# Scores of 64 queries by 192 keys with reversed sign, the sink as a 129th column, and decay factors from one maximum and four exponentials, in a two-layer hybrid attention and state-space trunk

## The chip, the cores and the metric

The kernel runs on one core of one Trainium2 chip. The metric is device time in microseconds (us), the median of the runs of one kernel. The engines are called as in the profile: PE is TensorE (matmuls), PEld its weight loads, DVE is VectorE, ACT is ScalarE, POOL is GpSimd, SP is SyncE, which issues all of this kernel's transfers.

## The reference, cut to what matters

One sequence of 2048 tokens of width 1024 goes through two layers. In each layer sixteen query heads (four key/value heads) attend to the last 128 tokens, with a learned sink in the softmax, beside a Mamba-2 scan in chunks of 128 tokens; both are gated and projected together.

```python
scores = jnp.einsum("bnqkgd,bnskd->bnkgqs", q, kb) * (HEAD_DIM ** -0.5)
scores = scores - slopes * dist                      # 128 queries x 256 keys, 128 of them valid
scores = jnp.where(valid, scores, -jnp.inf)
m = jnp.maximum(scores.max(axis=-1, keepdims=True), sink)
p = jnp.exp(scores - m)
probs = p / (p.sum(axis=-1, keepdims=True) + jnp.exp(sink - m))
out = jnp.einsum("bnkgqs,bnskd->bnqkgd", probs, vb)
attn = out * jax.nn.silu(z_attn)
...
diff = a_cs[..., :, None] - a_cs[..., None, :]       # a_cs: running sum of dt * a in a chunk
decay = jnp.exp(jnp.where(tril, diff, -jnp.inf))
y_diag = einsum(cb, decay, xdt)                      # per head, 128 x 128 decay factors
```

## The kernel before, in words

The work runs over 2 layers, 4 chunks of 512 tokens and 2 halves of the heads. A half has, in the order of the code, the key projection (`stage_k`), for each of its two key/value heads the query and gate projections (`proj_a`) and the attention (`mix_a`), the projections of the state-space group (`proj_s`), the output projection of the attention (`out_proj`) and the scan (`mix_s`); the output projection of the scan (`tail`) is put off until after the next `proj_a`. Numbers are split into a high and a low float32r part, so each projection is three matmuls of 512 columns (L229 to L231, L237 to L239, L448 to L450). The order on each engine is not written out by hand: a scheduler interleaves these stages when the program is built, and the engines then run their lists in that order.

`mix_a` works on blocks of 128 queries for four heads. There are 128 such blocks in the program. The scores of two heads go into one PSUM bank (`ps_s`; there is one buffer of it): per head two matmuls of 256 columns, the block's own 128 keys and the 128 before them (L376, L377). ACT copies the older half of both heads to an SBUF tile `e` (`s4`, L380) and DVE writes over it where the newer key is the valid one (L381), so that the 128 valid keys share 128 columns. Then DVE adds the distance term and takes the row maximum, head by head (L384), a small DVE operation forms the negated maximum with the sink (`nm`, L387), another the sink's distance from it (`es`, L389), ACT exponentiates that (L390) and the four heads (L393, with row sums `den`), DVE adds the sink's part to the sum (L395), inverts it (L396) and scales the tile (L397). PE transposes the four heads into `ps_pt` (L401); POOL separates the older from the newer keys (L409, L412), and four matmuls of 512 columns form the output (L416 to L419), which is gated by `zs` (L428, two operations).

`mix_s` works on 64 blocks. For each of two groups of four heads it loads the running sums of a block, one row per head, to all 128 partitions (L537, from the DRAM tile `a`, 2 KB to a partition), subtracts each partition's own sum and cuts at zero (L540, four operations on DVE), exponentiates (L542, one operation of 512 elements on ACT) and multiplies by `cbm` (L544, the first group on DVE and the second on POOL); `ps_yd` (L549) is the matmul that uses it. The tiles `e` of `mix_a` and `mix_s` share four buffers.

In the first layer's first chunk, weights are split as they come and stored; from the second chunk of the first layer on, `w_ahead` splits the weights of the second layer between other work (L103 on DVE, `whi` and `wr`).

Of the kernel before, what the change touches and what calls it, by code (L numbers as in the profile page):

```python
# [24 lines left out]
U8 = mybir.dt.uint8  # L25
# [28 lines left out]
def trunk(ctx, tc, a):  # L54
# [194 lines left out]
    def stage_vdt(L, lc, c, banks):  # L249
# [50 lines left out]
        nc.vector.tensor_copy(out=at, in_=ps[0:64, 128:256])  # L300
# [22 lines left out]
    def silu2(ps, name, pool, tag, bufs):  # L323
        th = tp.tile([P, 512], F32, name="th", bufs=1)
        nc.scalar.activation(out=th, in_=ps, func=AF.Tanh, scale=0.5)
        z = pool.tile([P, 512], F32, name=name, tag=tag, bufs=bufs)
# [3 lines left out]
    def proj_a(L, kv, X):  # L330
        qs, zs = [], []
        for j in range(2):
            ps = bank(ps_cm, "ps_q")
            proj_cm(X, L, 2 + kv * 2 + j, ps)
            q = ap_.tile([P, 2, CH], F32R, name="q", bufs=3)
            qf = q.bitcast(F32)
            u, v = slice(0, 64), slice(64, 128)
            nc.scalar.activation(out=q[u, 0], in_=ps[u], func=AF.Copy, scale=0.125)
            nc.scalar.activation(out=q[v, 1], in_=ps[v], func=AF.Copy, scale=0.125)
            nc.vector.scalar_tensor_tensor(out=q[v, 0], in0=ps[u], scalar=0.125, in1=qf[u, 0],  # L340
                                           op0=ALU.mult, op1=ALU.subtract)
            nc.vector.scalar_tensor_tensor(out=q[u, 1], in0=ps[v], scalar=0.125, in1=qf[v, 1],
                                           op0=ALU.mult, op1=ALU.subtract)
            qs.append(q)
        for j in range(2):
            ps = bank(ps_cm, "ps_z")
            proj_cm(X, L, 10 + kv * 2 + j, ps)
            zs.append(silu2(ps, "zsa", ap_, "zsa", 4))
# [9 lines left out]
    def mix_a(L, lc, c, kv, vr, vprev, kt, qs, zs, mixt):  # L358
        bias = ap_.tile([P, 4, P], F32, name="bias", bufs=1)
# [3 lines left out]
        for b in range(NB):  # L363
            first = c == 0 and b == 0
            s4 = tp.tile([P, 4, P], F32, name="e4", bufs=E4)
            if first:
                nc.gpsimd.memset(s4, NEG)
            blk = slice(b * P, (b + 1) * P)
            for j in range(2):
                ps = bank(ps_mx, "ps_s").rearrange("p (h u k) -> p h u k", h=2, u=2)  # L370
                for i in range(2):
                    if first:
                        ko, ks = ps[:, i, 1, :], slice(P, 2 * P)
                    else:
                        ko, ks = ps[:, i].rearrange("p u k -> p (u k)"), slice(b * P, b * P + 2 * P)
# [424 lines left out]
```

## Time and profile before

| | |
|---|---|
| time, median of 3 runs | 3267.14 us (3261.64 to 3271.08) |
| time of the profiled execution | 3269.05 us |
| its span, first to last instruction | 3267.3 us |
| busy: PE, PEld | 3133.6 us (96%), 2595.4 us (79%) |
| busy: DVE, ACT, POOL | 2315.4 us (71%), 1330.2 us (41%), 1187.6 us (36%) |
| mean granted TensorE clock | 0.984 |
| moved by DMA | 692.78 MB, mean 212 GB/s |

The span lies 1.75 us below the execution's own time. A busy share is an average over the whole span; matmuls overlap one another in the pipeline, so the busy time of PE holds some waiting too.

### The profile page before, as it was taken

How to read it: one execution, taken by the hardware profiler on the slowest of the kernel's cores; microseconds unless marked ns; L12 is line 12 of the kernel's file. 1: busy time of each engine (PE TensorE's matmuls, PEld its weight loads, DVE VectorE, ACT ScalarE, POOL GpSimd, SP SyncE). 2: the span in 40 equal slices, each digit the busy share in tenths (PEclk: the TensorE clock that was granted, in tenths of full speed). 3: DMA queues.
4: the chain of work that ended last, by engine and by line, in shares of the span. 5: the costliest groups of instructions: out<-in, count | busy, mean ns of one | idle time of the engine just before them, and what ended most of it. 6: DMA issues, size and time to landing. Idle time of an engine off the chain costs nothing.

```text
span 3267.3 us, 46525 instructions
## 1 busy us (share of the span) xinstructions
PE 3133.6 (96%) x15448; PEld 2595.4 (79%) x15448; DVE 2315.4 (71%) x5535; ACT 1330.2 (41%) x3607; POOL 1187.6 (36%) x1327
## 2 busy tenths in 40 slices
PE   9999899999999999999999999999999999999996
PEld 7788787787877878777888888887888878888885
DVE  6978778767687676876759666685766847678575
ACT  5646425344254442543424344252432425334341
POOL 2443442415334142441325414333253322444224
PEclk9999999999999999999999999999999999999997
DMA  8766769757698576985666455654457544565451
GB/s 305 232 244 229 249 223 306 258 172 260 220 296 279 179 233 222 308 288 185 217 194 224 155 173 187 200 197 164 161 191 233 172 157 163 182 228 171 158 198 66
DMA packets 261360, 692.78 MB, mean 212 GB/s; under 512 B 28928, under 2 KB 50176, under 8 KB 261120
## 3 DMA queue, kind: packets, MB, share of 16 engines
q1 hardware_dynamic: 261120, 689.82, 63.5%
q8 instruction: 122, 2.00, 0.3%
q14 instruction: 118, 0.97, 0.1%
HBM read 554.96 MB, written 134.74 MB: 211 GB/s over the span
## 4 chain that ended last, share of the span: by engine, by line
PE 55%; DVE 10%; DMA 9%; POOL 2%; issue 2%; ACT 2%; SPq 0%; DVEq 0%; ACTq 0%; POOLq 0%
PE ps_out L448 5%; PE ps_out L450 5%; PE ps_out L449 5%; PE ps_xbc L230 3%; PE ps_xbc L231 3%; PE ps_xbc L229 3%; DMA e<-a 2%; PE ps_yd L549 2%; PE ps_zs L237 2%; PE ps_zs L238 2%; PE ps_z L231 2%; PE ps_z L229 2%; PE ps_zs L239 2%; PE ps_z L230 2%; DMA wpair<-wd_o 2%
## 5 line engine op out<-in xcount | busy, mean ns | idle before, releaser
L448 PE MATMUL ps_out<-wpair,mixt 128*128 128x512 f32 x1008 | 406.3, 409 | 42.1 <-DMA wpair<-wd_o 21.7
L449 PE MATMUL ps_out<-wpair,mixt 128*128 128x512 f32 x1008 | 403.7, 401 | 7.8 <-DVE wpair L103 7.8
L450 PE MATMUL ps_out<-wpair,mixt 128*128 128x512 f32 x1008 | 401.0, 401 | 7.9 <-DVE mixt L103 5.1
L409 POOL TENSOR_SCALAR_AFFINE_SELECT gh<-fh 128x512 fp32r<-128x512 f32 x128 | 91.7, 716 | 619.6 <-ACT fh L98 583.1
L229 PE MATMUL ps_xbc<-xh,wpair 128*128 128x512 f32 x768 | 305.6, 398 | 0.0
L230 PE MATMUL ps_xbc<-xl,wpair 128*128 128x512 f32 x768 | 302.0, 393 | 0.0
L231 PE MATMUL ps_xbc<-xh,wpair 128*128 128x512 f32 x768 | 301.2, 392 | 0.0
L393 ACT ACTIVATE e<-e,nm 128x128 f32<-128x128 f32 x512 | 199.7, 391 | 181.5 <-DVE nm L387 181.1
L448 PEld LDWEIGHTS ps_out<-wpair,mixt 128*128 128x128 f32 x1008 | 194.8, 194 | 97.7 <-DMA wpair<-wd_o 27.2
L450 PEld LDWEIGHTS ps_out<-wpair,mixt 128*128 128x128 f32 x1008 | 195.1, 194 | 54.5 <-DVE mixt L103 7.8
L449 PEld LDWEIGHTS ps_out<-wpair,mixt 128*128 128x128 f32 x1008 | 195.7, 194 | 49.4 <-DVE wpair L103 10.7
L380 ACT COPY e<-ps_s 128x256 f32<-128x256 f32 x240 | 88.6, 369 | 336.0 <-PE ps_s L377 334.1
L540 DVE TENSOR_SCALAR e<-e,nacs 128x128 f32<-128x128 f32 x512 | 168.9, 392 | 73.7 <-DMA e<-a 73.1
L493 DVE SCALAR_TENSOR_TENSOR cacc<-ps_xbc,conv,cacc 128x511 f32<-128x511 f32 (+2 forms) x288 | 213.4, 741 | 9.9 <-ACT cacc L490 8.0
L237 PE MATMUL ps_zs<-wpair,xh 128*128 128x512 f32 x512 | 203.5, 400 | 7.5 <-DMA wpair<-wd_z 7.5
L355 POOL TENSOR_TENSOR vw<-vr,vw 128x64 fp32r<-128x64 f32 x152 | 62.7, 413 | 392.4 <-ACT vw L354 377.2
L239 PE MATMUL ps_zs<-wpair,xl 128*128 128x512 f32 x512 | 202.2, 395 | 0.0
L238 PE MATMUL ps_zs<-wpair,xh 128*128 128x512 f32 x512 | 201.7, 394 | 0.0
L229 PE MATMUL ps_z<-xh,wpair 128*128 128x512 f32 x512 | 201.4, 393 | 0.0
L230 PE MATMUL ps_q<-xl,wpair 128*128 128x512 f32 x512 | 201.3, 393 | 0.0
L231 PE MATMUL ps_z<-xh,wpair 128*128 128x512 f32 x512 | 201.2, 393 | 0.0
L229 PE MATMUL ps_q<-xh,wpair 128*128 128x512 f32 x512 | 201.0, 393 | 0.0
(227 smaller groups left out, 8396.4 us busy)
## 6 DMA issues: line engine op xcount, KB each, us to landing
wpair<-wd_cm SPq DMA_DIRECT2D x420, 512.0 KB, 3.6
wpair<-wd_o SPq DMA_DIRECT2D x221, 512.0 KB, 4.1
wpair<-wd_z SPq DMA_DIRECT2D x112, 512.0 KB, 3.9
e<-a SPq DMA_DIRECT2D x128, 256.0 KB, 4.4
wr<-wcm SPq DMA_DIRECT2D x120, 256.0 KB, 4.5
wd_cm<-wpair SPq DMA_DIRECT2D x60, 512.0 KB, 3.7
wr<-wo SPq DMA_DIRECT2D x64, 256.0 KB, 4.8
wd_o<-wpair SPq DMA_DIRECT2D x32, 512.0 KB, 3.7
```

What stands on the lines that cost most here:

```text
L229: nc.tensor.matmul(out=ps, lhsT=wh[:, s], rhs=xh, start=(k == 0), stop=False)
L230: nc.tensor.matmul(out=ps, lhsT=wh[:, s], rhs=xl, start=False, stop=False)
L231: nc.tensor.matmul(out=ps, lhsT=wl[:, s], rhs=xh, start=False, stop=(k == KT - 1))
L237: nc.tensor.matmul(out=banks[b], lhsT=xh[:, s], rhs=wh, start=(k == 0), stop=False)
L238: nc.tensor.matmul(out=banks[b], lhsT=xh[:, s], rhs=wl, start=False, stop=False)
L239: nc.tensor.matmul(out=banks[b], lhsT=xl[:, s], rhs=wh, start=False, stop=(k == KT - 1))
L393: nc.scalar.activation(out=s4[:, h, :], in_=s4[:, h, :], func=AF.Exp, bias=nm[:, h:h + 1], accum_out=den[:, h:h + 1])
L448: nc.tensor.matmul(out=banks[b], lhsT=mh, rhs=wh, start=(e == 0), stop=False)
L449: nc.tensor.matmul(out=banks[b], lhsT=mh, rhs=wl, start=False, stop=False)
L450: nc.tensor.matmul(out=banks[b], lhsT=ml, rhs=wh, start=False, stop=(e == 3))
L493: nc.vector.scalar_tensor_tensor(out=acc[:, m:], in0=ps[:, 0:CH - m], scalar=cw[:, j:j + 1], in1=acc[:, m:], op0=ALU.mult, op1=ALU.add)
L540: nc.vector.tensor_scalar(out=e4[:, h, :], in0=e4[:, h, :], scalar1=d["nacs"][:, q:q + 1], scalar2=0.0, op0=ALU.add, op1=ALU.min)
```

## The change

Four parts.

1. **Scores.** The queries are scaled by -0.125 and stored so that 64 queries of two heads lie side by side. A matmul then takes 64 queries of two heads (128 columns of weights) against the 192 keys that these queries can reach, where it took 128 queries of one head against 256 keys. There are eight of them a block, as before. A partition of `e` is now one query of one of two heads. Two ACT copies (L387, L388) take the place of one in the second half of the block, since the 64 newest columns there lie first; the masked copy of DVE (L389) covers 64 columns for each of two heads, where it covered 128.
2. **Sink.** `e` gets a 129th column, which POOL fills with the negated sink (L371, 128x4). The scores are negated, so one minimum over 129 columns gives `nm` (L393) and one exponential with scale -1 over 129 columns gives the whole row sum (L397). L387, L389, L390 and L395 of before go.
3. **Gate.** `zs` is one tile of two gates, and the gating one operation of 256 elements (L435) for two of 128.
4. **Decay.** The stored sums are negated. One DVE operation over 512 elements takes the maximum of the loaded sum and the partition's own (L546), and four ACT exponentials of 128 elements, with scale -1 and the partition's sum as bias (L548), take the place of the one without bias. Since rows of `e` are now 129 wide, L544 loads 512 bytes four times to a partition, for 2 KB once.

```diff
-            q = ap_.tile([P, 2, CH], F32R, name="q", bufs=3)
+            q = ap_.tile([P, CH // 64, 2, 64], F32R, name="q", bufs=3)
...
-            s4 = tp.tile([P, 4, P], F32, name="e4", bufs=E4)
+            s5 = tp.tile([P, 4, P + 1], F32, name="e4", bufs=E4)
+            s4 = s5[:, :, 0:P]
...
+            nc.gpsimd.tensor_copy(out=s5[:, :, P:], in_=ns.unsqueeze(2))
             blk = slice(b * P, (b + 1) * P)
-            for j in range(2):
-                ps = bank(ps_mx, "ps_s").rearrange("p (h u k) -> p h u k", h=2, u=2)
-                for i in range(2):
...
-                    nc.tensor.matmul(out=ko, lhsT=qs[j][:, i, blk], rhs=kt[:, 0, ks], start=True, stop=False)
-                    nc.tensor.matmul(out=ko, lhsT=qs[j][:, i, blk], rhs=kt[:, 1, ks], start=False, stop=True)
-                sj = s4[:, 2 * j:2 * j + 2, :]
-                if not first:
-                    nc.scalar.copy(out=sj, in_=ps[:, :, 0, :])
-                nc.vector.copy_predicated(out=sj, mask=low.unsqueeze(1).broadcast_to([P, 2, P]), data=ps[:, :, 1, :])
-            m = sm.tile([P, 4], F32, name="m")
+            sv = s4.rearrange("p (s j) c -> p s j c", s=2)
+            for s in range(2):
+                t0 = b * P + s * 64
+                ps = bank(ps_mx, "ps_s")[:, 0:384].rearrange("p (j k) -> p j k", j=2)
+                o0 = 128 - 64 * s if first else 0
+                for j in range(2):
+                    for part in range(2):
+                        nc.tensor.matmul(out=ps[:, j, o0:], lhsT=qs[j][:, t0 // 64].rearrange("p i q -> p (i q)"),
+                                         rhs=kt[:, part, t0 + o0:t0 + 192], start=(part == 0), stop=(part == 1))
+                own, other = slice(64 * s, 64 * s + 64), slice(64 - 64 * s, 128 - 64 * s)
+                if not first and s == 0:
+                    nc.scalar.copy(out=sv[:, s], in_=ps[:, :, 0:128])
+                elif s == 1:
+                    if not first:
+                        nc.scalar.copy(out=sv[:, s, :, own], in_=ps[:, :, 0:64])
+                    nc.scalar.copy(out=sv[:, s, :, other], in_=ps[:, :, 64:128])
+                nc.vector.copy_predicated(out=sv[:, s, :, own], mask=low.unsqueeze(1).broadcast_to([P, 2, 64]),
+                                          data=ps[:, :, 128:192])
+            nm = sm.tile([P, 4], F32, name="nm")
             for h in range(4):
-                nc.vector.tensor_tensor_reduce(out=s4[:, h, :], in0=s4[:, h, :], in1=bias[:, h, :], scale=1.0,
-                                               scalar=-3.0e38, op0=ALU.add, op1=ALU.max, accum_out=m[:, h:h + 1])
-            nm = sm.tile([P, 4], F32, name="nm")
-            nc.vector.scalar_tensor_tensor(out=nm, in0=m, scalar=-1.0, in1=ns, op0=ALU.mult, op1=ALU.min)
-            es = sm.tile([P, 4], F32, name="es")
-            nc.vector.tensor_tensor(out=es, in0=nm, in1=ns, op=ALU.subtract)
-            nc.scalar.activation(out=es, in_=es, func=AF.Exp)
+                nc.vector.tensor_tensor_reduce(out=s5[:, h, :], in0=s5[:, h, :], in1=bias[:, h, :], scale=1.0,
+                                               scalar=3.0e38, op0=ALU.add, op1=ALU.min, accum_out=nm[:, h:h + 1])
...
-                nc.scalar.activation(out=s4[:, h, :], in_=s4[:, h, :], func=AF.Exp, bias=nm[:, h:h + 1],
+                nc.scalar.activation(out=s5[:, h, :], in_=s5[:, h, :], func=AF.Exp, scale=-1.0, bias=nm[:, h:h + 1],
                                      accum_out=den[:, h:h + 1])
-            nc.vector.tensor_tensor(out=den, in0=den, in1=es, op=ALU.add)
...
-            for j in range(2):
-                nc.vector.tensor_tensor(out=t[:, j, :], in0=t[:, j, :], in1=zs[j][:, blk], op=ALU.mult)
+            nc.vector.tensor_tensor(out=t, in0=t, in1=zs[:, :, blk], op=ALU.mult)
...
-                e4 = tp.tile([P, 4, P], F32, name="e4", bufs=E4)
+                e4 = tp.tile([P, 4, P + 1], F32, name="e4", bufs=E4)[:, :, 0:P]
...
+                nacs = d["nacs"][:, r0:r0 + 4]
+                nc.vector.tensor_tensor(out=e4, in0=e4, in1=nacs.unsqueeze(2).broadcast_to([P, 4, P]), op=ALU.max)
                 for h in range(4):
-                    q = b * 16 + g * 8 + u * 4 + h
-                    nc.vector.tensor_scalar(out=e4[:, h, :], in0=e4[:, h, :],
-                                            scalar1=d["nacs"][:, q:q + 1], scalar2=0.0, op0=ALU.add, op1=ALU.min)
-                nc.scalar.activation(out=e4, in_=e4, func=AF.Exp)
+                    nc.scalar.activation(out=e4[:, h, :], in_=e4[:, h, :], func=AF.Exp, scale=-1.0, bias=nacs[:, h:h + 1])
```

The rest of the diff follows from these: the views in which POOL separates older and newer keys have runs of 64, the views of `ps_o` are rearranged, and the tables of distances and sinks are laid out for the new rows.

The scheduler makes a new order of the whole program. On DVE, a block's softmax in the second half of a state-space projection stands so before (L384 is shown as ISA, its second row reads the row result out; the L103 row is a weight split that has nothing to do with the block):

```order
L381 COPY_PREDICATED e_13405<-low,ps_s 128x256
L384 ISA e_13405,m<-e_13405,bias 128x128
L384 ISA m 128x1
L384 ISA e_13405,m<-e_13405,bias 128x128
L384 ISA m 128x1
L387 SCALAR_TENSOR_TENSOR nm<-m,nsink 128x4
L103 TENSOR_TENSOR wr<-wr,whi 128x512
L389 TENSOR_TENSOR es<-nm,nsink 128x4
L395 TENSOR_TENSOR den<-den,es 128x4
L396 RECIPROCAL den<-den 128x4
L397 SCALAR_TENSOR_TENSOR e_13405<-e_13405,den 128x512
```

and so in the changed kernel:

```order
L389 COPY_PREDICATED e_13142<-low,ps_s 128x2x64
L393 ISA e_13142,nm<-e_13142,bias 128x129
L393 ISA nm 128x1
L393 ISA e_13142,nm<-e_13142,bias 128x129
L393 ISA nm 128x1
L103 TENSOR_TENSOR wr<-wr,whi 128x512
L399 RECIPROCAL den<-den 128x4
L400 SCALAR_TENSOR_TENSOR e_13142<-e_13142,den 128x4x128
```

Three small operations are gone, and only the weight split still stands between the row result and the reciprocal.

On ACT, the decay factors of a block stand so before (L98 are casts of the scan and of the next output projection's input, L587 the sum of squares of the scan's output):

```order
L430 CAST mixt<-yy 128x256
L542 ACTIVATE e_26460<-e_26460 128x512
L542 ACTIVATE e_26468<-e_26468 128x512
L98 CAST fh<-xx 128x512
L587 ACTIVATE th,ssq<-yy 128x512
L98 CAST gh<-st_103 128x512
```

and so in the changed kernel, at a like place:

```order
L98 CAST fh<-xx 128x512
L548 ACTIVATE e_23986<-e_23986,nacs 128x128 x4
L548 ACTIVATE e_23994<-e_23994,nacs 128x128 x4
L593 ACTIVATE th,ssq<-yy 128x512
L98 CAST gh<-st_104 128x512
L98 CAST mixt<-ps_g 128x512
```

Eight short calls stand where two long ones stood, ahead of the same casts.

On PE, a group of four score matmuls stands within a state-space projection before:

```order
L376 MATMUL ps_s<-kt,q 128x256
L417 MATMUL ps_o<-gl,vw 64x512
L377 MATMUL ps_s<-kt,q 128x256
L376 MATMUL ps_s<-kt,q 128x256
L377 MATMUL ps_s<-kt,q 128x256
L231 MATMUL ps_xbc<-xh_12200,wpair 128x512
```

and in the changed kernel:

```order
L380 MATMUL ps_s<-kt,q 128x192 x2
L424 MATMUL ps_o<-gl,vw 64x512
L380 MATMUL ps_s<-kt,q 128x192 x2
L229 MATMUL ps_xbc<-xh_3752,wpair 128x512
L230 MATMUL ps_xbc<-xl_3753,wpair 128x512
```

The groups are as long as before, with 192 columns for 256. What lies between them has moved: counted over the 128 blocks, the median number of matmuls between a block's last score matmul and its first transposition is 50 before and 42 in the changed kernel.

## Rows read from the trace of the kernel before

**Rows 1.** Page, part 1: busy time, share of the span, instructions.

```profile
PE 3133.6 (96%) x15448; PEld 2595.4 (79%) x15448; DVE 2315.4 (71%) x5535; ACT 1330.2 (41%) x3607; POOL 1187.6 (36%) x1327
```

**Rows 2.** Cores: span and mean granted TensorE clock.

```profile
core 0: 3267.3 us, clock 0.984
```

**Rows 3.** Windows: length, busy PE, PEld, DVE, ACT, POOL (instructions), clock, DMA share, GB/s.

```profile
900.00:1300.00 400.00, 377.40 (x1816) 310.46 (x1815) 278.41 (x680) 165.76 (x436) 131.29 (x149) 0.97 0.73 243
2100.00:2500.00 400.00, 394.31 (x1986) 329.86 (x1985) 277.26 (x697) 154.53 (x437) 150.12 (x171) 1.00 0.56 183
```

**Rows 4.** Waits of PE: total us, times, longest us.

```profile
PE ps_out L448 <- DMA wpair<-wd_o: 21.7, 19, 3.3
PE ps_out L449 <- DVE wpair L103: 7.8, 6, 2.8
PE ps_out L448 <- ACT mixt L98: 7.7, 8, 3.0
...
PE ps_pt L401 <- DVE e L397: 5.6, 11, 1.0
...
PE ps_q L231 <- DVE wpair L103: 0.2, 1, 0.2
PE ps_out L448 <- ACT wpair L98: 0.2, 1, 0.2
```

**Rows 5.** Timeline of PE around a score group of 256 columns: start us, us, instruction.

```profile
457.43 0.28 PE L376 MATMUL ps_s<-kt,q 128*128 128x256 f32 x1
...
457.90 0.40 PE L229 MATMUL ps_q<-xh,wpair 128*128 128x512 f32 x1
458.14 0.40 PE L230 MATMUL ps_q<-xl,wpair 128*128 128x512 f32 x1
```

**Rows 6.** Timeline of PE around a first block's group, of 128 columns.

```profile
39.98 0.22 PE L376 MATMUL ps_s<-kt,q 128*128 128x128 f32 x1
...
40.66 0.40 PE L230 MATMUL ps_q<-xl,wpair 128*128 128x512 f32 x1
```

**Rows 7.** Timeline of the weight loads of that group.

```profile
40.09 0.19 PEld L376 LDWEIGHTS ps_s<-kt,q 128*128 128x128 f32 x1
40.20 0.19 PEld L377 LDWEIGHTS ps_s<-kt,q 128*128 128x128 f32 x1
```

**Rows 8.** Groups of DVE by form: count, busy us, mean ns, idle before.

```profile
L540 DVE TENSOR_SCALAR e<-e,nacs 128x128 f32<-128x128 f32 x512 | 168.9, 392 | 73.7 <-DMA e<-a 73.1
L381 DVE COPY_PREDICATED e<-low,ps_s 128x256 f32<-128x256 uint8 x256 | 112.7, 440 | 67.0 <-ACT e L380 62.9 <-PE ps_s L377 1.2
...
L428 DVE TENSOR_TENSOR yy<-yy,zsa 128x128 f32<-128x128 f32 x256 | 76.5, 340 | 0.9
...
L544 DVE TENSOR_TENSOR e<-e,cbm 128x512 f32<-128x512 f32 x64 | 48.9, 764 | 2.5 <-ACT e L542 2.1
...
L389 DVE TENSOR_TENSOR es<-nm,nsink 128x4 f32<-128x4 f32 x128 | 43.2, 337 | 2.9
...
L387 DVE SCALAR_TENSOR_TENSOR nm<-m,nsink 128x4 f32<-128x4 f32 x128 | 32.0, 250 | 1.9
...
L395 DVE TENSOR_TENSOR den<-den,es 128x4 f32<-128x4 f32 x128 | 27.4, 214 | 95.3 <-ACT e L393 90.7 <-ACT es L390 4.1 <-ACT halo L498 0.3
```

**Rows 9.** Groups of ACT by form.

```profile
L393 ACT ACTIVATE e<-e,nm 128x128 f32<-128x128 f32 x512 | 199.7, 391 | 181.5 <-DVE nm L387 181.1
...
L380 ACT COPY e<-ps_s 128x256 f32<-128x256 f32 x240 | 88.6, 369 | 336.0 <-PE ps_s L377 334.1
L542 ACT ACTIVATE e<-e 128x512 f32<-128x512 f32 x128 | 80.8, 631 | 214.1 <-DVE e L540 188.2 <-issue 10.5 <-PE ps_yo L563 5.9
...
L390 ACT ACTIVATE es<-es 128x4 f32<-128x4 f32 x128 | 24.8, 194 | 0.7 <-DVE es L389 0.7
```

**Rows 10.** DMA issues: count, KB each, median us to landing.

```profile
e<-a SPq DMA_DIRECT2D x128, 256.0 KB, 4.4
...
wpair<-wd_v SPq DMA_DIRECT2D x56, 272.0 KB, 3.5
```

More of the change, by code (lines that the diff above doesn't have):

```diff
@@ L299, in stage_vdt @@
         at = sm.tile([64, P], F32, name="acsT", bufs=1)
-        nc.vector.tensor_copy(out=at, in_=ps[0:64, 128:256])
+        nc.vector.tensor_scalar(out=at, in0=ps[0:64, 128:256], scalar1=-1.0, scalar2=None, op0=ALU.mult)
         nc.sync.dma_start(out=a_dram[L][c], in_=at)
@@ L321, in stage_k, with silu2 @@
         return kts
-    def silu2(ps, name, pool, tag, bufs):
+    def silu2(ps, z):
         th = tp.tile([P, 512], F32, name="th", bufs=1)
         nc.scalar.activation(out=th, in_=ps, func=AF.Tanh, scale=0.5)
-        z = pool.tile([P, 512], F32, name=name, tag=tag, bufs=bufs)
         nc.vector.scalar_tensor_tensor(out=z, in0=th, scalar=1.0, in1=ps, op0=ALU.add, op1=ALU.mult)
@@ L330, in proj_a @@
     def proj_a(L, kv, X):
-        qs, zs = [], []
+        qs = []
+        zs = ap_.tile([P, 2, CH], F32, name="zsa", bufs=2)
         for j in range(2):
@@ L358, in mix_a @@
     def mix_a(L, lc, c, kv, vr, vprev, kt, qs, zs, mixt):
-        bias = ap_.tile([P, 4, P], F32, name="bias", bufs=1)
+        bias = ap_.tile([P, 4, P + 1], F32, name="bias", bufs=1)
         nc.sync.dma_start(out=bias, in_=a["bias"][kv])
@@ L514, in proj_s @@
             proj_tok(X, banks, k, wh, wl)
-        o["zs"] = [silu2(banks[b], "zss", sp, "zss", 4) for b in range(NB)]
+        o["zs"] = [silu2(banks[b], sp.tile([P, 512], F32, name="zss", bufs=4)) for b in range(NB)]
         return o
@@ L699, in trunk @@
     nc.vector.memset(ones, 1.0)
-    low = const.tile([P, P], U8, name="low")
-    nc.vector.tensor_copy(out=low, in_=w_load(a["low"], P))
+    low = const.tile([P, 64], U8, name="low")
+    nc.vector.tensor_copy(out=low, in_=w_load(a["low"], 64))
     mhalf = const.tile([P, NB], F32, name="mhalf")
@@ L767, in _layout @@
     rows = np.concatenate([np.asarray(t, f) for t in (dt_bias, a_log, d_skip, sinks)], 1)
-    A["rows"] = np.broadcast_to(rows[:, None, :], (DEPTH, P, 64))
+    rows = np.repeat(rows[:, None, :], P, 1)
+    sk = np.asarray(sinks, f).reshape(DEPTH, 4, 2, 2).transpose(0, 3, 1, 2)
+    sk = np.broadcast_to(sk[:, :, None, :, None, :], (DEPTH, 2, 64, 4, 2, 2))
+    rows[:, :, 48:64] = sk.reshape(DEPTH, P, 16)
+    A["rows"] = rows
     cv = np.concatenate([np.asarray(conv_w, f), np.asarray(conv_b, f)[:, None, :]], 1)
@@ L778, in _layout @@
     i = np.arange(P)
-    dist = ((i[:, None] - i[None, :]) % P).astype(f)
-    A["bias"] = (-(slopes.reshape(4, 1, 4, 1) * dist[None, :, None, :])).astype(f)
+    dist = ((i[:, None] - i[None, :]) % P).astype(f).reshape(2, 64, P).transpose(1, 0, 2)
+    bias = (slopes.reshape(4, 2, 2).transpose(0, 2, 1)[:, :, None, None, :, None] * dist[None, None, :, :, None, :])
+    A["bias"] = np.pad(bias.reshape(4, P, 4, P), ((0, 0), (0, 0), (0, 0), (0, 1))).astype(f)
     A["triu"] = (i[:, None] <= i[None, :]).astype(f)
-    A["low"] = (i[None, :] <= i[:, None]).astype(f)
+    A["low"] = (i[None, 0:64] <= i[:, None] % 64).astype(f)
     r = np.arange(P)
```

34 lines of the change are left out of this document (17 added, 17 removed).

## The prediction

> **What bounds the kernel now.** I read the busy shares first. PE is busy for 3133.6 us of the span, DVE for 71% of it, ACT for 41% [rows 1, 2]. So PE's own list sets the time, and the question is where its 133.7 us of idle time (3267.3 less 3133.6) comes from, since an engine beside it can only matter through that. Next come the windows. In the stretch from 900 to 1300 us, where the second layer's weights are split beside the first layer's work, PE is idle for 22.6 of 400 us at a granted clock of 0.97; in the second layer, from 2100 to 2500, for 5.7 us at 1.00, with DVE as busy in both [rows 3]. The reader is to see that the second layer has hardly anything to win, and that idle time is followed by a lower clock. Over the span the clock is 0.984 [rows 2], so 1.6% of 3267.3, 52 us, is lost by matmuls at the lower of the two levels.
>
> The list of PE's waits says who ends them. No row is above 22 us; the largest is a weight transfer. DVE ends 15 of the 32 rows, from 7.8 us down to 0.2, together 49.6 us; ACT ends seven, from 7.7 down to 0.2, together 22.8 us [rows 4]. Most of these are operands of the output projections. The softmax itself is nearly out of sight: PE waits for the scaled probabilities in only 11 of 128 blocks, for 5.6 us in all.
>
> **The change part by part.** The sum is made against the profiled execution's 3269.05 us, which lies 1.9 us above the median of 3267.14.
>
> *Score matmuls.* A group of four with 256 columns and the following matmul of 512 take from 457.43 to 458.14, 0.71 us [rows 5]. The same with 128 columns, in the first block, takes from 39.98 to 40.66, 0.68 us [rows 6]. The 192 columns lie between, so each of the 240 groups outside the first blocks gains between 0 and 0.03 us, 0 to 7.2 us in all. Why so little for half the columns: the weight loads of the short group follow one another every 0.11 us [rows 7], and the 256-column matmuls every 0.12 (0.47 us from 457.43 to 457.90, by four). There are still eight weight loads a block. By the slope between 256 and 512 columns (0.24 less 0.1175, by 256: 0.48 ns a column) 192 columns would need 0.087 us, less than the 0.11 of a weight load; so the load sets the pace, as it does at 128, and I take 7 us off.
>
> Against this stands a rule of the Trainium skill, page "TensorE: Matmul & The Clock Gate", section "Back-to-back issue gap": warm matmuls follow one another at N / 2.4 + 2.5 ns. By it 64 columns less are 26.7 ns, over 960 matmuls an estimated 26 us. The same formula gives 56 ns at 128 columns, and rows 6 and 7 show 0.11 us, so the trace does not agree for this mix of float32r loads and matmuls; the sum goes by the rows.
>
> *DVE.* The decay arguments take 512 operations of 392 ns, 168.9 us. One operation over 512 elements with two inputs from SBUF is L544 at 764 ns, so 128 of them are 97.8 us: 71.1 us less. The masked copy halves from 256 to 128 elements; from L428 (128 elements, 340 ns) to L544 (512, 764) is 1.10 ns an element, so 141 ns each, 36 us over 256. Gating goes from 256 x 340 ns to 128 x 481 ns on the same line: 14.9 us less. The three small operations go: 32.0, 43.2 and 27.4, together 102.6 us [rows 8]. The sum is 225 us: DVE falls from 2315 to 2091 us. What of it reaches PE is the unknown; the bounds are nothing (PE waited for something else just behind) and all 49.6 us. I take the share by how long work queues on an engine that is busy for a share r, r / (1 - r): from 0.709 to 2091 / 3250 = 0.643 it falls from 2.43 to 1.80, by 26%. Of 49.6 us that is 12.9 us off.
>
> *ACT.* The decay factors cost one call of 631 ns before (80.8 us) and four of 128 elements with a bias, as L393, of 391 ns now: 512 x 391 = 200.2 us, so 119 us more. The copies from PSUM become, per block, one of 369 ns and two of half the size; a half lies between 185 and 369 ns, I take 277, which is 22 us more over 120 blocks. The sink's exponential goes, 24.8 us [rows 9]. ACT rises by 117 us to 1447, from 0.407 to 0.445 of the span; its queue grows from 0.69 to 0.80, by 17%, and of the 22.8 us that ACT ends this gives 3.9 us back. The bounds are 0 and 22.8.
>
> *The rest.* The loads of the sums have four times the rows to write. The nearest row is a load of 272 KB in twice as many pieces, which lands in 3.5 us, against 4.4 for the 256 KB of sums [rows 10]; I take nothing. If landing doubled, the 73.1 us that DVE is idle for these loads [rows 8] would double too, a third of what DVE gains, and 4 us would come back. The sink column is a POOL copy of 128x4. No row of POOL has that size; the bounds are nothing and the dearest small row, 337 ns, 43 us on an engine that is busy for 36% [rows 1, 8]. It needs only a free buffer, and where it came late DVE's minimum would wait, and with it all that stands behind on DVE; the program places the copies ahead of POOL's separations of earlier blocks, so I take nothing.
>
> *The clock.* PE's idle time falls by 12.9 - 3.9 = 9.0 us, 6.7% of 133.7. If the 52 us of low clock shrink with it, that is 3.5 us more; bounds 0 and 52 x 49.6 / 133.7 = 19.
>
> *Sum.* 3269 - 7 - 12.9 + 3.9 - 3.5 = 3249.5 us, and 1.9 less for the median: **3248 us**.
>
> **The rivals.**
>
> *Columns count in full.* If 192 columns cost their 0.087 us, 960 matmuls gain 0.031 us each, 29 us for 7, and the time is **3226 us**. The slope of rows 5 speaks for it; rows 6 speak against it, where 128 columns took nearly as long as 256. This is what the rule of the Trainium skill above would do, by its own figure 3229. Chance 0.07.
>
> *No change.* PE is fed by transfers and by its own order, and the DVE work taken out was spare: only the shorter score groups are left, less 4 us given back by ACT. That is 3267 - 7 + 4 = **3264 us**. For it speaks that the largest wait is a transfer, and the stretch from 2100 to 2500 us with 5.7 us of idle time under the same DVE load; against it the many small DVE rows in the list. Chance 0.25.
>
> *Slower: the transpositions are called too early.* The new order puts eight matmuls fewer between a block's last score and its first transposition, 8 x 0.24 = 1.9 us. What the rows take off the chain there is nm (0.25), the sink's sum (0.21) and 0.14 of the masked copy, 0.60 us. If nothing else shortens it, the probabilities are 1.3 us later by PE's clock, and PE, which does its list in order, waits with all projections queued behind. Eleven blocks in 128 have no margin now; if a quarter of the blocks lose 1.3 us, that is 42 us, and the time **3290 us**. It decides the sign from 12% of the blocks on (19.5 us by 128 x 1.3). Against it speaks that small operations queue too: every one of the three that go is a place where other DVE work, as the weight split in the listing, came between. Chance 0.18.
>
> **How the numbers follow.** The forecast has 0.50, with a range of its own from 3230 (DVE's waits more than halved) to 3262 (a tenth of them gone, ACT's up by a third). A measurement of this kernel can tell a difference of about 0.3%, 10 us, from none; so faster means below 3257, slower above 3277. Faster: most of the forecast (0.46), the columns (0.07) and a lucky part of "no change" (0.06), 0.59. Slower: the early transpositions, 0.18. The rest, 0.23, is the same. The range reaches from 3205, the columns in full and twice the gain from DVE with its clock, to 3290.
>
> **What would show it.** In the changed profile the decay maximum should take about 0.76 us and its four exponentials 0.39 each; DVE should be busy for about 2090 us and ACT for about 1450; score groups of 192 columns with the next matmul should span 0.68 us, not 0.60 (the columns in full) or 0.71. PE's waits ended by DVE should be near 37 us in all, those by ACT near 27. The early transpositions would show as a row of L404 waiting for L400 of 20 us or more. The forecast is wrong if DVE is lighter but the same waits reappear under another name, above all under transfers, or if the loads of the sums, now in pieces of 512 bytes, land so late that the scan's matmul waits.

## The result and the profile after

The changed kernel took **3227.45 us** (median of 4 runs, 3224.55 to 3236.11), the kernel before on the same chip 3267.74 (4 runs, 3261.64 to 3271.08). The ratio is 0.9881, with a 95% interval from 0.9864 to 0.9898: 40 us or 1.2% faster. The forecast was 3248 in a range from 3205 to 3290.

The profiled execution took 3224.55 us. Part 1 of its page (busy time, share, instructions), to be read against [rows 1]:

```profile
PE 3112.1 (97%) x15448; PEld 2582.7 (80%) x15448; DVE 2137.7 (66%) x4639; ACT 1419.3 (44%) x3991; POOL 1228.6 (38%) x1455
```

Its span and granted clock, as in [rows 2], and the two windows of [rows 3]:

```profile
core 0: 3222.8 us, clock 0.987
```

```profile
900.00:1300.00 400.00, 380.93 (x1861) 311.59 (x1860) 273.10 (x587) 177.03 (x494) 143.18 (x171) 0.98 0.74 247
2100.00:2500.00 400.00, 396.40 (x2007) 331.91 (x2006) 262.81 (x589) 170.33 (x493) 159.93 (x196) 1.00 0.58 189
```

The span is 44.5 us shorter. PE's idle time went from 133.7 to 110.7 us (3222.8 less 3112.1), 23 us. The loss to the lower clock, the span times what the mean clock lacks to 1, went from 52.3 us (1.6% of 3267.3) to 41.9 (1.3% of 3222.8), 10.4 us. The remaining 11 us are in PE's busy time beyond that. In both windows PE is idle for less: by 3.5 us in the first, by 2.1 in the second.

How far such a split can be trusted is shown by a second trace of the changed program: the run `reorder_after` below turned out to be the same program, with the same order on every engine. Its span and the first part of its page:

```profile
core 0: 3223.5 us, clock 0.990
```

```profile
PE 3103.7 (96%) x15448; PEld 2576.6 (80%) x15448; DVE 2133.0 (66%) x4639; ACT 1419.3 (44%) x3991; POOL 1229.7 (38%) x1455
```

The span is the same within 1 us, but PE is idle for 119.8 us where it was 110.7, and the loss to the clock is 32.2 us where it was 41.9. So of the gain, idle time is 14 to 23 us and the clock 10 to 20. The clock can also be averaged over all executions that have it on record: 65 of the kernel before lost 50 us in the mean, eight of the changed program 38. That is 12 us of the gain.

PE's waits, answering to [rows 4] (total us, times, longest us):

```profile
PE ps_out L455 <- DMA wpair<-wd_o: 27.2, 17, 6.2
PE ps_g L596 <- POOL yy L591: 9.0, 8, 1.7
PE ps_st L583 <- DVE fl L103: 7.5, 8, 3.0
...
PE ps_out L457 <- DVE mixt L103: 2.9, 3, 1.2
...
PE ps_out L455 <- ACT mixt L437: 2.4, 4, 1.3
...
PE ps_pt L404 <- DVE e L400: 1.2, 3, 0.5
```

The whole list, added up by the engine that ended the wait, was 49.6 us for DVE and 22.8 for ACT before, and is 26.0 and 13.5 now. POOL's went from 7.8 to 14.8, the transfers' from 33.6 to 35.8. These sums vary too: the second trace of the changed program has 25.3, 15.9, 13.3 and 44.7, and the null swap below, which does the work of the kernel before, has 39.3 for DVE and 18.9 for ACT. So the fall of DVE's lies between 13 and 24 us and that of ACT's between 3 and 9. The transposition (L404) waits less than it did.

A score group with the matmuls behind it, as in [rows 5] (start us, us, instruction):

```profile
457.13 0.58 PE L380 MATMUL ps_s<-kt,q 128*128 128x192 f32 x4
457.55 0.41 PE L229 MATMUL ps_q<-xh,wpair 128*128 128x512 f32 x1
457.81 0.40 PE L230 MATMUL ps_q<-xl,wpair 128*128 128x512 f32 x1
```

From 457.13 to 457.81 are 0.68 us, what the 128-column group took [rows 6], and 0.03 less than 256 columns. Over all groups of four that stand in one piece the median is 0.677 us (217 groups), and 0.706 us (198) in the kernel before.

The groups of DVE that the change touched, answering to [rows 8] (count, busy us, mean ns, idle time before):

```profile
L546 DVE TENSOR_TENSOR e<-e,nacs 128x512 f32<-128x512 f32 x128 | 108.0, 846 | 110.5 <-DMA e<-a 109.9
...
L389 DVE COPY_PREDICATED e<-low,ps_s 128x128 f32<-128x128 uint8 x256 | 77.2, 301 | 85.2 <-ACT e L388 53.7 <-ACT e L384 26.6 <-PE ps_s L380 2.8
...
L435 DVE TENSOR_TENSOR yy<-yy,zsa 128x256 f32<-128x256 f32 x128 | 62.1, 485 | 1.4
```

And of ACT, the decay's exponentials, answering to [rows 9]:

```profile
L548 ACT ACTIVATE e<-e,nacs 128x128 f32<-128x128 f32 x512 | 164.2, 392 | 219.7 <-DVE e L546 208.2 <-PE ps_v L239 6.0 <-PE ps_yo L569 5.2
```

The prices came as forecast: 301 ns for 299, 485 for 481, 392 for 391; the maximum took 846 ns for 764. DVE fell by 178 us, where the parts by their rows (169 - 108, 113 - 77, 77 - 62, and 103 for the three small operations that are gone) make 213: other DVE work grew by 35. A busy time of DVE is itself good to some 20 us only: the null swap has 2295.4 us for the operations that took 2315.4 before.

Two of ACT's own waits; then the second one as it was before, with PE's wait for the same conversion (now 2.4 us, above):

```profile
ACT e L548 <- DVE e L546: 208.2, 94, 10.3
...
ACT mixt L437 <- DVE yy L435: 51.1, 56, 2.3
```

```profile
ACT mixt L430 <- DVE yy L428: 90.0, 73, 3.2
...
PE ps_out L448 <- ACT mixt L430: 5.7, 7, 1.1
```

### The profile page after: what moved, and what is told of

It is laid out like the page before. It is cut to its first block, busy times and chain, and to the rows that moved or that the text cites. A ratio compares the mean times of both kernels' runs of the same rounds, so it can differ in the third digit from the quotient of the medians.

```text
span 3222.8 us, 46551 instructions
## 1 busy us (share of the span) xinstructions
PE 3112.1 (97%) x15448; PEld 2582.7 (80%) x15448; DVE 2137.7 (66%) x4639; ACT 1419.3 (44%) x3991; POOL 1228.6 (38%) x1455
## 4 chain that ended last, share of the span: by engine, by line
PE 74%; DMA 13%; DVE 5%; POOL 4%; issue 2%; ACT 2%; SPq 1%; DVEq 0%; ACTq 0%; POOLq 0%
PE ps_out L455 6%; PE ps_out L457 6%; PE ps_out L456 6%; PE ps_xbc L229 4%; PE ps_xbc L231 4%; PE ps_xbc L230 4%; PE ps_z L231 3%; PE ps_z L229 3%; PE ps_z L230 3%; PE ps_q L229 3%; PE ps_q L231 3%; PE ps_q L230 3%; PE ps_s L380 3%; PE ps_yd L555 3%; DMA e<-a 2%; DMA wpair<-wd_o 2%
## 5 line engine op out<-in xcount | busy, mean ns | idle before, releaser
L397 ACT ACTIVATE e<-e,nm 128x129 f32<-128x129 f32 x512 | 203.2, 399 | 225.0 <-DVE nm L393 221.0
L548 ACT ACTIVATE e<-e,nacs 128x128 f32<-128x128 f32 x512 | 164.2, 392 | 219.7 <-DVE e L546 208.2
L393 DVE CUSTOM_DVE_ANT_0 e<-e,bias 128x129 f32<-128x129 f32 x512 | 199.4, 426 | 7.7 <-DMA bias<-bias 2.3
L229 PE MATMUL ps_q<-xh,wpair 128*128 128x512 f32 x512 | 201.2, 393 | 0.2
L230 PE MATMUL ps_z<-xl,wpair 128*128 128x512 f32 x512 | 201.2, 393 | 0.0
L231 PE MATMUL ps_q<-xh,wpair 128*128 128x512 f32 x512 | 200.7, 392 | 0.2 <-DVE wpair L103 0.2
```

The source lines that it names most:

```text
L229: nc.tensor.matmul(out=ps, lhsT=wh[:, s], rhs=xh, start=(k == 0), stop=False)
L230: nc.tensor.matmul(out=ps, lhsT=wh[:, s], rhs=xl, start=False, stop=False)
L231: nc.tensor.matmul(out=ps, lhsT=wl[:, s], rhs=xh, start=False, stop=(k == KT - 1))
L393: nc.vector.tensor_tensor_reduce(out=s5[:, h, :], in0=s5[:, h, :], in1=bias[:, h, :], scale=1.0, scalar=3.0e38, op0=ALU.add, op1=ALU.min, ...
L397: nc.scalar.activation(out=s5[:, h, :], in_=s5[:, h, :], func=AF.Exp, scale=-1.0, bias=nm[:, h:h + 1], accum_out=den[:, h:h + 1])
```

## The experiments

Four theories were set against each other. *Load*: TensorE is late because operands queue on VectorE, so the time follows the work on VectorE. *Chain*: the time follows the length of the way from scores to transposition. *ScalarE's queue*: ACT's added work takes part of the gain back. *Order*: the program's order on each engine is planned afresh for every variant, and the new one happens to be better.

How much the order moved is given as follows, from the built programs. TensorE's list is cut into stretches, matmuls in a row that write a tile of one name (2275 in the changed kernel). Two lists are laid side by side, and the stretches counted that find no partner of the same name and length in the same order. From before to after 1603 moved. The count is generous: the longest order that both lists have in common leaves out 1166. So no part of the change can be added with everything else left in place. Against the changed kernel the counts of the runs below are 925 for 256 columns, 1111 without the decay part, 1383 and 117 for the two loads on VectorE, 1409 for the scaling on ScalarE and 108 for the sink's copy there; against the kernel before, 699 for the decay part alone, 1893 for the sink's column, 1507 for the layout and 0 for the null swap.

### The columns alone

```
-  ps = bank(ps_mx, "ps_s")[:, 0:384].rearrange("p (j k) -> p j k", j=2)
+  pw = bank(ps_mx, "ps_s").rearrange("p (j k) -> p j k", j=2)
...
-  rhs=kt[:, part, t0 + o0:t0 + 192], ...
+  rhs=kt[:, part, b * P + o0:b * P + 256], ...
```

> The changed kernel with the score matmuls over 256 columns again (64 queries of two heads, all 256 keys, of which 192 are read). If the weight loads set the pace at 192 columns, a group of four with the next matmul goes from 0.68 to 0.71 us, 240 groups give back 7 us: about 3235 us. If the shorter matmuls are a main part of the gain (the rival in which columns count in full), 25 to 30 us come back: about 3255 us. If only the order of the schedule matters, anything within 20 us of 3227.

Measured 3248.06 us (3236.81 to 3250.67; ratio to before 0.9925, 0.9904 to 0.9946). Part 1 of its page, and the same place in its timeline:

```profile
PE 3119.8 (96%) x15448; PEld 2590.6 (80%) x15448; DVE 2132.7 (66%) x4639; ACT 1424.7 (44%) x3991; POOL 1229.6 (38%) x1455
```

```profile
458.32 0.64 PE L380 MATMUL ps_s<-kt,q 128*128 128x256 f32 x4
458.80 0.40 PE L230 MATMUL ps_q<-xl,wpair 128*128 128x512 f32 x1
459.03 0.40 PE L231 MATMUL ps_q<-xh,wpair 128*128 128x512 f32 x1
```

The time lies between the 3235 us of the weight loads and the 3255 of the columns. From 458.32 to 459.03 are 0.71 us again (the median over 226 groups is 0.706), and PE is busy for 7.7 us more than after, about the 7.2 us of the prediction's working. But the span (3245.3 us) is 22.5 us longer; the other 14.8 are idle time, in good part ended by DVE (40.6 us for 26.0) and ACT (22.1 for 13.5), though both have the work they had. This order differs from the changed kernel's in 925 stretches. I meant to repeat it in another order:

```
+  wcur = v_window(vr[b], kv)
   pt = bank(ps_mx, "ps_pt")
...
-  wcur = v_window(vr[b], kv)
```

> 256 columns again, with the value window's loading ahead of the transpositions, an order that left the changed kernel's time as it was. 256 columns gave back 20 us, where the spacing of groups (0.71 against 0.68 us) explains 7. If the other 13 us belong to the columns: 3248 again. If they belong to the order in which that program happened to run: about 3236, the changed kernel and 7 us.

> The changed kernel with the loading and splitting of a value window placed ahead of the transpositions in the code: the same instructions on every engine, TensorE's in another order. If the gain lies in the work that the engines have: 3227 give or take 5. Order-and-layout theory (the order that the change happened to get is a good one, any other gives the gain back): 3240 to 3265.

Measured 3246.20 (3240.36 to 3254.33) with 256 columns and 3229.49 (3225.22 to 3231.88) with 192. The edit did not do what these expectations say: moving the lines left the order on every engine as it was. So both are repeats: they show that 256 columns are slower each time (by 20.6 and by 16.7 us), and say nothing of another order. How the difference is made up is less stable. In the repeats' traces PE's busy time differs by 15.9 us (3119.6 and 3103.7) and its idle time by 6.3 (126.1 and 119.8). What holds is the spacing of the groups: 240 times 0.029 us are 7 us for the columns. The mean loss to the clock is 45.7 us over the 12 executions with 256 columns and 37.9 over the eight with 192, another 8. Whether that and the few us left come from the order planned for 256 columns or from PE's being later at each group is open.

### The parts

The decay part alone on the kernel before, and the change without it, by the same edit forwards and back:

```
-  for h in range(4):
-      nc.vector.tensor_scalar(out=e4[:, h, :], in0=e4[:, h, :],
-                              scalar1=d["nacs"][:, q:q + 1], scalar2=0.0, op0=ALU.add, op1=ALU.min)
-  nc.scalar.activation(out=e4, in_=e4, func=AF.Exp)
+  nc.vector.tensor_tensor(out=e4, in0=e4, in1=nacs.unsqueeze(2).broadcast_to([P, 4, P]), op=ALU.max)
+  for h in range(4):
+      nc.scalar.activation(out=e4[:, h, :], in_=e4[:, h, :], func=AF.Exp, scale=-1.0, bias=nacs[:, h:h + 1])
```

> The kernel before with the decay part alone (negated sums, one maximum, four exponentials with bias; rows of the tile stay 128 wide, so the loads stay in pieces of 2 KB). DVE-load theory: DVE saves about 61 of the 178 us, ACT has 83 us more; a third of the gain that is not columns, 11 us, so about 3257 us. Softmax-chain theory (what counts is how soon a block's probabilities are there, not how busy DVE is): no gain, 3264 to 3272 us, since the decay chain is not shorter. ACT-queue theory (four short calls cost more than they free): slower, 3275 us or more.

> The changed kernel with the decay part undone (four subtractions cut at zero on DVE, one exponential). DVE-load theory: DVE busy for about 2200 us, 11 us of the gain lost, about 3238 us. Softmax-chain theory: nothing lost, 3222 to 3232 us. If the decay part costs on ACT what it saves on DVE: 3227 us or a little less, as with the chain theory; the waits of PE ended by ACT then fall below 13 us.

Measured 3256.13 (3243.76 to 3261.16; ratio 0.9953, 0.9937 to 0.9970) and 3236.19 (3229.18 to 3238.29; 0.9888, 0.9866 to 0.9910). The decay part is worth 13 us on the kernel before, which took 3269.32 in that set of runs, and 9 on the rest of the change; but the second ratio, 0.9888, is hardly apart from the whole change's 0.9881, so those 9 us are not shown. Both times are near what the load theory expected, but its reason is not to be seen: with the decay part alone DVE's busy time fell by 23 us (to 2291.9) where 61 were expected, little more than the null swap's 20, while ACT's rose by 78 (to 1408.3).

The sink's column with negated scores, and the 64 x 192 layout, each alone on the kernel before:

```
+  nc.gpsimd.tensor_copy(out=s5[:, :, P:], in_=ns.unsqueeze(2))
...
-  nc.vector.scalar_tensor_tensor(out=nm, in0=m, scalar=-1.0, in1=ns, op0=ALU.mult, op1=ALU.min)
-  nc.vector.tensor_tensor(out=es, in0=nm, in1=ns, op=ALU.subtract)
-  nc.scalar.activation(out=es, in_=es, func=AF.Exp)
...
-  nc.vector.tensor_tensor(out=den, in0=den, in1=es, op=ALU.add)
```

> The kernel before with the negated scores and the sink as a 129th column alone. Takes the three small operations of a block (250, 337 and 214 ns, 102 us in all) off VectorE; matmuls and the decay part as before. VectorE-load theory (the gain goes with VectorE's busy time, about 33 us for 178 us of it): about 19 us, 3250. Softmax-chain theory (the gain is the shorter way from scores to transposition): most of the gain of the change without its columns, some 30 us, 3240. Order-and-layout theory (what is gained does not follow the work): anything within 10 us of 3264.

> The kernel before with the 64-query x 192-key scores alone: positive scores, sink, gate and decay as before. Takes the columns (7 us by the 0.71 to 0.68 us of a group) and about 35 us of VectorE's predicated copies away. VectorE-load theory: 7 + 35/178 x 33 = 13 us, 3256. Softmax-chain theory: 7 us for the columns, the chain is as long as before: 3262. Order-and-layout theory: anything within 10 us of 3262.

Measured 3243.83 (3234.91 to 3254.58; ratio 0.9924, 0.9904 to 0.9943) and 3257.00 (3248.86 to 3262.12; 0.9960, 0.9947 to 0.9974), beside 3268.80. The sink's column is the largest part, 25 us; it lies between what load (19) and chain (30) expected. The layout gives 12 us, about the 13 of the load theory, with DVE at 2294.9 us, 20 less, which again is no more than the null swap shows. 25 + 12 + 13 are 50 us where the whole gave 40. The gate part was not run alone.

A run for the size of chance, two independent copies and two independent additions of the kernel before in the other order:

```
-  nc.scalar.copy(out=t[u], in_=pv[v, :, 0, :])
   nc.scalar.copy(out=t[v], in_=pv[u, :, 1, :])
+  nc.scalar.copy(out=t[u], in_=pv[v, :, 0, :])
```

> The kernel before with two independent copies and two independent additions in another order in the code, which changes no work and lets the scheduler make a new order. It measures what a new order alone does. If the gain has a cause in the work: within 10 us of 3267. If the gain of 40 us is a lucky order: differences of 15 us or more from 3267 are to be expected here, of either sign.

Measured 3260.62 (3255.98 to 3266.03; ratio 0.9972, 0.9959 to 0.9984). Part 1 of its page:

```profile
PE 3132.2 (96%) x15448; PEld 2597.3 (80%) x15448; DVE 2295.4 (70%) x5535; ACT 1330.3 (41%) x3607; POOL 1201.5 (37%) x1327
```

So a difference of 0.3% or 9 us can come from nothing that the theories speak of. The decay part and the layout, each alone, are hardly above it; the sink's column and the whole are. But the run does not show what its expectation meant it to, the effect of a new order: the operations stand in the same order on every engine, only the halves are swapped. No run measures a new order alone, so it may have a part in each of these gains.

### Work put back on VectorE

```
+  scr = sm.tile([P, P], F32, name="scr", bufs=1)
+  for n in range(4):
+      nc.vector.tensor_tensor(out=scr, in0=bias[:, n, 0:P], in1=bias[:, n, 1:], op=ALU.add)
   den = sm.tile([P, 4], F32, name="den")
```

> The changed kernel with four additions of 128x128 put in on VectorE in each attention block, behind the reductions, into a tile that nobody reads: about 174 us of VectorE's time, as much as the change takes off it, and nothing put on the way from scores to transposition except where the next VectorE instruction queues behind them. VectorE-load theory: about 30 us of the gain is given back, 3255. Softmax-chain theory: VectorE waits there for ScalarE's exponentials anyway (4 x 400 ns), the additions hide, 3227 to 3233. Order-and-layout theory: 3227 give or take 10.

Measured 3271.67 us (3265.60 to 3278.90; ratio 1.0014, 1.0002 to 1.0025): the whole gain is gone, more than the load theory's 30 us. Part 1 of its page, then waits of PE, then one of ACT's (total us, times, longest us):

```profile
PE 3134.6 (96%) x15448; PEld 2591.6 (79%) x15448; DVE 2290.5 (70%) x5151; ACT 1421.6 (43%) x3991; POOL 1239.4 (38%) x1455
```

```profile
PE ps_out L458 <- ACT mixt L440: 9.1, 6, 2.6
...
PE ps_out L460 <- DVE mixt L103: 8.0, 6, 2.2
PE ps_out L458 <- ACT mixt L98: 7.3, 8, 2.6
```

```profile
ACT mixt L440 <- DVE yy L438: 88.1, 63, 5.6
```

DVE is busy for 153 us more than after, nearly as much as the change took off. The waits that it ends went from 26.0 to 51.4 us. Those that *ACT* ends went from 13.5 to 31.6, with ACT's work the same (1421.6 us for 1419.3). The last row shows a way: ACT's conversion of the gated output waits for DVE's `yy` for 88.1 us, where it waited 51.1 after the change and 90.0 before, and PE's wait for this conversion went from 2.4 to 9.1 us. These 6.7 of the 18.1 us are best read as DVE's lateness, handed on; the rest is not traced back. The clock fell to 0.982, a loss of 58.9 us for 41.9; with 24.3 us more of idle time (135.0 for 110.7) that is 41 of the 47 us by which the span grew. (VectorE also stood 18.9 us for the distance table that the additions read, which makes it a little later still.)

The order had moved too, in 1383 stretches, so the run doesn't tell work from order. For that I looked for work that leaves the order nearly alone:

```
+  scr = sm.tile([P, 4], F32, name="scr", bufs=1)
+  nc.vector.tensor_tensor(out=scr, in0=ns[:, 0:4], in1=ns[:, 0:4], op=ALU.add)    (six times)
```

> The changed kernel with six additions of 128x4 on VectorE in each attention block, behind the reductions, into a tile that nobody reads: 6 x 128 x about 200 to 250 ns (the small operations took 214 to 337 ns) = 154 to 192 us of VectorE's time, as much as the four additions of 128x128 whose run gave back 44 us. Those had moved TensorE's order as well: of 2275 stretches of matmuls into one tile, 1383 stood in another order than in the changed kernel; with these six, 117 do. VectorE-load theory (the work itself holds TensorE up): 35 to 44 us given back again, 3262 to 3271. Order theory (what the additions of 128x128 cost came by the other order): 3227 to 3237. Both in part: between.

Measured 3275.28 us (3270.28 to 3284.27; ratio 1.0028, 1.0017 to 1.0040), slower than either theory expected. The windows from 60 to 500 us and from 500 to 3000, of after first and then of this kernel (columns as in [rows 3]):

```profile
60.00:500.00 440.00, 426.06 (x2089) 353.71 (x2089) 316.12 (x646) 227.11 (x603) 187.73 (x213) 0.98 0.71 239
500.00:3000.00 2500.00, 2440.71 (x12173) 2027.72 (x12172) 1660.29 (x3621) 1086.28 (x3098) 956.86 (x1140) 0.99 0.66 214
```

```profile
60.00:500.00 440.00, 395.33 (x1868) 314.45 (x1867) 408.51 (x1244) 209.99 (x554) 156.08 (x178) 0.97 0.65 212
500.00:3000.00 2500.00, 2433.19 (x12135) 2019.62 (x12134) 1661.69 (x3650) 1079.53 (x3096) 959.10 (x1145) 0.99 0.67 216
```

The additions need nothing from a block, and the program put them nearly all into the first 500 us: 1244 DVE instructions there for 646, and no more than usual later. In that stretch DVE is busy for 93% of the time (408.51 of 440), and PE, with nearly the order of the changed kernel, does 1868 matmuls for 2089. Later, with DVE as it was, PE is nearly as it was. So work on VectorE costs TensorE time with hardly a change of TensorE's order; but this shows it for an engine that is almost full, not for 70% against 66% over the whole span. How much of the 44 us of the run before this one is work, and how much order, stays open.

### Work moved to ScalarE

```
-  nc.vector.scalar_tensor_tensor(out=s4, in0=s4, scalar=0.5, in1=den.unsqueeze(2)..., ...)
+  for h in range(4):
+      nc.scalar.activation(out=s4[:, h, :], in_=s4[:, h, :], func=AF.Copy, scale=den[:, h:h + 1])
...
-  split(ph, pl, pt.rearrange("p (h q) -> p h q", h=4), "act")
+  nc.scalar.activation(out=ph, in_=pq4, func=AF.Copy, scale=0.5)
+  nc.vector.scalar_tensor_tensor(out=pl, in0=pq4, scalar=0.5, in1=ph.bitcast(F32), ...)
```

> The changed kernel with the scaling by the inverse denominators on ScalarE: four copies of 128x128 with a scale for each row take the place of VectorE's one operation of 128x512 (785 ns, 100 us in all), and the factor 0.5 goes into the two operations that split the transposed result. ScalarE gets 128 x 4 x 275 to 392 ns = 141 to 200 us more, and the way from the scores to the transposition gets 0.3 to 0.8 us longer. VectorE-load theory, with the 44 us that 174 us of VectorE's work have cost: 100 x 0.25 = 25 us faster than the changed kernel, 3202. Softmax-chain theory: the longer way costs some 10 us, 3237. Total-work theory (work on any engine that TensorE waits for counts alike): 10 to 25 us slower, 3245.

Measured 3243.35 us (3241.66 to 3245.74; ratio 0.9919, 0.9907 to 0.9931), 16 us slower than the changed kernel. Part 1 of its page, one row of PE's waits, and the group that was moved:

```profile
PE 3126.3 (96%) x15448; PEld 2590.9 (80%) x15448; DVE 2075.3 (64%) x4511; ACT 1575.4 (49%) x4503; POOL 1218.9 (38%) x1455
```

```profile
PE ps_pt L404 <- ACT e L401: 8.5, 6, 2.2
```

```profile
L401 ACT ACTIVATE e<-e,den 128x128 f32<-128x128 f32 x512 | 164.5, 392 | 27.0 <-DVE den L399 26.2
```

The load theory in its plain form expected 3202 and misses by 41 us; only a new order that costs as much could save it. DVE is 62 us lighter, yet the waits that it ends are the same (26.4 us for 26.0), and those ended by ACT rose from 13.5 to 25.4: the transposition waits for the four scaled copies, which keep ACT busy for 1.29 us a block (164.5 us by 128) where DVE took 0.785. The expectation for work that counts on either engine, 3245, was met. But the longer way is not shown to be what costs the 16 us: PE's whole idle time is 117.4 us, between the 110.7 and the 119.8 of the changed program. What grew is the loss to the clock, 49.3 us in the mean of the five executions for 37.9.

The other move, of the sink's column from POOL to ACT:

```
-  nc.gpsimd.tensor_copy(out=s5[:, :, P:], in_=ns.unsqueeze(2))
+  nc.scalar.copy(out=s5[:, :, P:], in_=ns.unsqueeze(2))
```

> The changed kernel with the copy of the sink column on ScalarE, in front of its own copies of scores into the same tile, rather than on GpSimd, which stands behind that copy for 311 us in all, up to 24 us at a time. If TensorE's waits for GpSimd (14.8 us, against 7.8 before the change) come from it: some 7 us faster, 3220. If GpSimd's waiting there covers other waiting: no change, 3227, or up to 5 us slower by ScalarE's 128 further operations of about 200 ns.

Measured 3225.32 us (3224.33 to 3231.14; ratio 0.9862, 0.9848 to 0.9877), no change, with nearly the same order. POOL's waits, of after and then of this kernel:

```profile
POOL e L371 <- PE ps_pt L404: 310.6, 36, 24.3
...
POOL gh L416 <- ACT fh L98: 236.4, 95, 9.0
```

```profile
POOL gh L416 <- ACT fh L98: 556.6, 95, 25.3
```

POOL stood behind the copy for 311 us in all, up to 24 us at a time; without the copy it stands that long at the next operation of its list, the separation of the keys, which waits for the transposed probabilities. PE's waits for POOL are 13.3 us for 14.8. A long wait was moved along POOL's list at no price.

## Why the prediction came out as it did

**The bound and the direction** were right: PE's list sets the time, and what there was to win lay in PE's waits and in the clock. The size was not: 19 us were forecast and 40 measured. The median lies in the wide range, but 3 us outside the forecast's own one (3230 to 3262).

**Scores, -7 us.** Right: 0.68 us a group, and 0.029 us less than with 256 columns in the median, 7 us in all. The rival of columns in full would have shown 0.60 us. The four matmuls of a group follow one another every 0.106 us in the changed kernel and every 0.118 before, where the prediction's slope gave 0.087 for 192 columns. The formula that it quotes (the Trainium skill, page "TensorE: Matmul & The Clock Gate", section "Back-to-back issue gap") gives an estimate of 0.083 us. The section states it for an isolated matmul and says that in a stream of weight loads and matmuls both set the spacing, which the prediction left out; the traces at 128, 192 and 256 columns agree with that. The rival's time, 3226, is next to the one measured; it would have been reached for a wrong reason.

**DVE, -12.9 us.** The direction held, the size did not: waits ended by DVE fell by 23.6 us in the profiled executions, by 13 to 24 with the other traces. The failing step is the share, 26% by r / (1 - r) over the busy share of the span. By the busy time that DVE really lost (178, not 225 us; 0.709 to 0.663) it would have been 19%, against the 48% measured, or 34% from the null swap's 39.3. (The gate's 14.9 us come from the row's 76.5 us; the 256 x 340 ns of the text would be 87.0. The row measured 14.4 less.) The queue formula treats VectorE as one queue with the span's mean load, and one run speaks against that: scaling on ACT lost time with a lighter DVE. That an operand's lateness depends on all that it passes would fit this, and also that the sink's column, which takes three operations and one of ACT out of one way from scores to output, gave the largest part of the gain. It is not shown: the order moved in both runs, and the sink's column alone also takes most off DVE's busy time (to 2199.5 us).

**ACT, +3.9 us.** Wrong sign: ACT got 89 us more work (117 were forecast, but the four exponentials of a group overlap: 512 x 392 ns are 201 us, and the group is busy for 164.2), and the waits that it ends fell from 22.8 to 13.5. The prediction read the engine that ended a wait as its cause. The conversion of the gated output contradicts that: its own wait for DVE fell from 90.0 to 51.1 us with the change and PE's wait for it from 5.7 to 2.4, and both came back when DVE alone got work (88.1 and 9.1), though in another order. So a part of ACT's waits is VectorE's, passed on.

**The rest, 0.** Loads in smaller pieces landed in 4.2 us for 4.4 [rows 10]. DVE stood idle for them longer (109.9 us for 73.1), which cost nothing that a run shows. The sink's copy was priced at nothing; PE's waits for POOL rose by 7 us, which the prediction didn't have, but taking the copy off POOL gave nothing back.

**The clock, -3.5 us.** Too small: 12 us in the mean of all executions. In the profiled pair idle time fell by 17% and the loss by 20%, as if the prediction's rule (in proportion to idle time) held. That was luck: the second trace of the changed program has more idle time (119.8 us) and less loss (32.2), and the layout alone loses 57.8 us in the mean of its eight executions with 131.0 us of idle time, where the kernel before loses 50 with 133.7. What sets the loss stays open.

**The sum.** Of the terms, -7, -9 and -3.5 were forecast for the columns, the waits and the clock. The profiled pair shows -23 of idle time and -10.4 of clock in -44.5; with the columns' 7, some 4 us are left in PE's busy time and not settled. With the second trace idle time is -14 and the clock -20. *No change* (3264) fell with the waits. *Transpositions too early* (3290) fell with L404's row: 1.2 us of waiting in 3 blocks, for 5.6 in 11.

**What stays open.** The order on TensorE moved in 1603 stretches. No run held the order and changed the load by the change's own amount over the whole span, so the part of the order in the 40 us isn't known. That 256 columns cost 17 to 21 us, of which the columns themselves are 7, says that it may be more than a few. No run here is faster than the changed kernel by more than the measurement can tell.

## What to carry to other kernels

When one engine's list bounds a kernel, look behind the engine that ended a wait: follow its own waits one step further before its work is priced, since lateness is handed on (PE's wait for one conversion of ACT's went from 2.4 to 9.1 us when only DVE got work). Do not price a lighter engine by its busy share alone: here the forecast so made had half the gain, and 62 us off DVE at ACT's expense gained nothing. Count the granted clock with the rest, over many executions: it was 12 of the 40 us. And trace one program twice before a split of its time into waits, work and clock is believed, since here two traces of equal length differ by some 10 us in each.

## What the runs showed of the hardware

- Two programs with the same operations in the same order on every engine, which differ only in which of two halves comes first, stood 0.28% apart (interval 0.16 to 0.41%).
- Two executions of one program had spans of 3222.8 and 3223.5 us, but PE idle for 110.7 and 119.8 us and mean granted clocks of 0.987 and 0.990: the one with more idle time had the higher clock.
- A copy on ACT of 128x128 with a scale for each row took 392 ns, as much as an exponential of that size with a bias; a plain copy of that size out of PSUM took 275.
- VectorE's 128x4 additions took 0.16 us in the median in the stretch where they crowd, but 0.22 to 0.29 in the mean, with single ones at 1.3 us.
- A maximum of 128x512 over a tile whose rows lie 129 apart took 846 ns in the changed kernel and 903, 947 and 960 in three of the variants, with the same operands, and 891 with rows 128 apart; the nearest row before was 764 ns [rows 8].
